# Six buffers of split weights placed 64 bytes apart modulo 512 in a float32r transformer trunk

## The chip, the cores and the metric

The kernel runs on one core of a Trainium2 chip. The metric is the device time of one execution in microseconds (us); the median of several runs is compared. Engines are named as the profile names them: PE multiplies matrices (PEld is its weight load, which overlaps), DVE, ACT and POOL work elementwise, SP issues the loads.

## What is computed

The reference is a decoder trunk of two pre-norm layers on 256 tokens of width 2048, all in float32. Layer 0 mixes tokens by sliding-window attention with sinks, layer 1 by a sparse attention with compressed, selected and window branches. Both have the same frame:

```python
def mixer_a(h, w_in, sinks, w_out, cos, sin):
    proj = h @ w_in
    q, k, v, z = jnp.split(proj, [A_WIDTH, A_WIDTH + A_KV_WIDTH, A_WIDTH + 2 * A_KV_WIDTH], axis=-1)
    ...
    return (o * jax.nn.silu(z)) @ w_out

def reference(...):
    for i in range(DEPTH):
        h = rmsnorm(x, norm_w[i])
        ...
        x = x + out.astype(x.dtype)
    return rmsnorm(x, final_norm_w)
```

The four big products (two `w_in`, two `w_out`) and the small compression network (mlp) of layer 1 read every weight once.

## The kernel before

Float32 products are made of float32r matmuls on operands split in two: `hi` is the value rounded to float32r, `lo` the rest. Weights come in steps of 128 x 1024 floats: SP loads one into `raw` (4 buffers), ACT writes `w_hi`, DVE writes `w_lo = raw - w_hi` (`split`, lines 558 to 569; 3 buffers each, the six buffers of this case), and PE uses both. The activations are split likewise into `hT` (the normed input) and `aT_hi`, `aT_lo` (the mixer's gated output).

A step is used in one of three ways. In "tok" steps (`add_steps`) a 128-column slice of `hT` or `aT` is the stationary operand and 512 columns of `w_hi`, `w_hi` again, and `w_lo` stream past it: three matmuls of 512 columns for each of two slices of tokens and two rows of weights. In "feat" steps (the gate z) the weights are stationary, 128 columns at a time, and `hT` streams: one matmul of 512 columns on `w_hi`, one of 256 on `w_lo`. The mlp streams 256 columns of weights past slices of `X`, which lie 488 bytes apart, and the attention scores stream `kTA` or `kTB` past `qT`. A row of `kTA` takes 2112 bytes (4 x 512 + 64), so its eight rows (four groups, hi and lo) start 64 bytes apart modulo 512, while `qT` starts at one fixed place.

Nothing is issued as it is written. Each call is recorded as an operation with the boxes of the tiles that it touches (`record`); two operations depend on each other where boxes overlap (`_overlap`). `order` then runs a list scheduler with estimated costs over all of them and writes the program in the order of its start times. For a slice of a tile the box is exact; for a slice of a slice `View.__getitem__` keeps the box of the first slice. The semaphores of the built program are made later from the real addresses.

`place` fixes where tiles lie: rings of tiles whose rows are a multiple of 512 bytes come first, from the longest to the shortest, then the others as they were recorded. So in the kernel before every tile with a row of 512 bytes or a multiple, the six weight buffers, `raw`, `hT`, `aT`, `kTA` and `qT` among them, starts at the same place modulo 512.

The first two steps are split in two halves each (`parts = 2`), since PE waits for them at the start; all others in one piece.

Of the kernel before, what the change touches and what calls it, by code (L numbers as in the profile page):

```python
# [13 lines left out]
F32R = mybir.dt.float32r  # L14
# [6 lines left out]
P = 128  # L21
# [318 lines left out]
def trunk(ctx: ExitStack, tc: tile.TileContext, x, final_norm_w, a_w_in, a_w_out, b_w_in, kc_pos, kc_w1, kc_w2, vc_pos, vc_w1, vc_w2,  # L340
# [5 lines left out]
    sb = Ring(plan, ctx.enter_context(tc.tile_pool(name="sb", bufs=1)))  # L346
# [15 lines left out]
    def copy(out, in_, scale=1.0):  # L362
        return ACT.activation(out, in_, AF.Copy, scale=scale)
# [195 lines left out]
    def split(st):  # L559
        n = st.cols  # L560
        plan.early = FIRST
        st.hi, st.lo = st.room() if hasattr(st, "room") else (
            sb.tile([P, 1024], F32R, tag=tag, name=tag, bufs=3) for tag in ("w_hi", "w_lo"))
        parts = 2 if st.idx < 2 else 1
        for c in range(parts):
            part = slice(c * n // parts, (c + 1) * n // parts)
            st.ops = (copy(st.hi[:, part], st.raw[:, part]),
                      DVE.tensor_sub(st.lo[:, part], st.raw[:, part], st.hi[:, part]))
        plan.early = 0
# [761 lines left out]
    for i in range(AHEAD):  # L1331
        split(steps[i])
    rates = [(0, 450.0), (nA, 900.0), (nA + 8, 600.0), (nA_out, 750.0), (nB, 1200.0)]
    for i, st in enumerate(steps):
        for start, r in rates:
            if i == start:
                state["rate"] = r
        if i == nA_out:
            mlp_loads()
        if i == nA + 8:  # L1340
            queue.append(pipeline(units, b_front, b_back))
        if i == 0:
            load_x(2)
        if i + LOADS < n:
            load(steps[i + LOADS])
        if i < 3:
            load_x((i + 3) % 4, steps[i + LOADS].load)
        if i + AHEAD < n:
            split(steps[i + AHEAD])
        for h in st.halves[:1] if i >= n - KT // 2 else st.halves:  # L1350
            h()
            background()
# [61 lines left out]
```

## Time and profile before

| | |
|---|---|
| median of 3 runs | 783.36 us (782.95 to 784.16) |
| the profiled execution | 783.71 us |
| its span in the profile | 781.6 us |
| PE busy | 767.5 us of the span (98%) |
| DVE, ACT, POOL busy | 569.7, 469.7, 123.5 us |

[...] Columns of each view are told where it first stands.

### The profile page before, as it was taken

How to read it: one execution, taken by the hardware profiler on the slowest of the kernel's cores; microseconds unless marked ns; L12 is line 12 of the kernel's file. 1: busy time of each engine (PE TensorE's matmuls, PEld its weight loads, DVE VectorE, ACT ScalarE, POOL GpSimd, SP SyncE). 2: the span in 40 equal slices, each digit the busy share in tenths (PEclk: the TensorE clock that was granted, in tenths of full speed). 3: DMA queues.
4: the chain of work that ended last, by engine and by line, in shares of the span. 5: the costliest groups of instructions: out<-in, count | busy, mean ns of one | idle time of the engine just before them, and what ended most of it. 6: DMA issues, size and time to landing. Idle time of an engine off the chain costs nothing.

```text
span 781.6 us, 11575 instructions
## 1 busy us (share of the span) xinstructions
PE 767.5 (98%) x3988; PEld 624.1 (80%) x3988; DVE 569.7 (73%) x1159; ACT 469.7 (60%) x950; POOL 123.5 (16%) x170
## 2 busy tenths in 40 slices
PE   8999999999999999999999999999999999999995
PEld 5888688788787788888888888878878887768884
DVE  5758959859779655556776479969969798965572
ACT  6847556457466444554666477657757866845442
POOL 1112112113023000020001020311132411111110
PEclk9999999999999999999999999999999999999998
DMA  9764454654553555666677664545445353464652
GB/s 326 241 187 137 140 185 110 182 176 127 172 176 116 184 185 187 188 191 176 188 241 234 169 170 116 155 115 156 120 131 141 109 160 104 131 193 150 195 168 107
DMA packets 86474, 129.73 MB, mean 166 GB/s; under 512 B 6322, under 2 KB 43233, under 8 KB 86288
## 3 DMA queue, kind: packets, MB, share of 16 engines
q1 hardware_dynamic: 85648, 127.16, 54.1%
q0 software_dynamic: 336, 1.29, 0.5%
q8 instruction: 31, 0.51, 0.3%
q10 hardware_dynamic: 432, 0.56, 0.2%
q14 instruction: 27, 0.22, 0.1%
HBM read 126.89 MB, written 2.10 MB: 165 GB/s over the span
## 4 chain that ended last, share of the span: by engine, by line
PE 83%; DVE 12%; issue 3%; DMA 1%; ACT 0%; ACTq 0%; POOLq 0%; POOL 0%; DVEq 0%
PE acc L217 68%; PE pv L217 4%; DVE w_lo L217 3%; PE s L217 3%; PE pT L217 3%; DVE sm L217 3%; DVE den L217 2%; DVE u L217 1%; PE mlp L217 1%; DVE qT L217 1%; PE qT L217 1%; PE gates L217 1%; PE xT L217 1%; DMA raw<-in_a_w_in 1%; DVE pt L217 1%
## 5 line engine op out<-in xcount | busy, mean ns | idle before, releaser
L217 DVE TENSOR_TENSOR w_lo<-raw,w_hi 128x1024 fp32r<-128x1024 f32 (+1 forms) x231 | 298.6, 1295 | 140.2 <-ACT w_hi L217 137.7
L217 ACT ACTIVATE w_hi<-raw 128x1024 fp32r<-128x1024 f32 (+1 forms) x231 | 241.1, 1048 | 161.5 <-PE acc L217 124.1
L217 PE MATMUL acc<-w_hi,hT 128*128 128x512 f32 x768 | 245.6, 396 | 2.8 <-ACT w_hi L217 1.8
L217 PE MATMUL acc<-hT,w_hi 128*128 128x512 f32 x512 | 185.0, 397 | 0.0
L217 PEld LDWEIGHTS acc<-w_hi,hT 128*128 128x128 f32 x768 | 142.5, 189 | 34.8 <-ACT w_hi L217 3.0
L217 PE MATMUL acc<-w_lo,hT 128*128 128x512 f32 x384 | 150.9, 395 | 0.0
L217 PE MATMUL acc<-hT,w_lo 128*128 128x256 f32 x512 | 144.8, 285 | 0.0
L217 PEld LDWEIGHTS acc<-hT,w_hi 128*128 128x128 f32 x512 | 96.2, 188 | 18.0
L217 PEld LDWEIGHTS acc<-hT,w_lo 128*128 128x128 f32 x512 | 96.6, 189 | 0.7
L217 PE MATMUL acc<-w_hi,aT_hi 128*128 128x512 f32 x236 | 92.5, 393 | 0.3 <-DVE kTB L217 0.3
L217 PE MATMUL acc<-w_hi,aT_lo 128*128 128x512 f32 x236 | 92.6, 392 | 0.0
L217 PE MATMUL acc<-w_lo,aT_hi 128*128 128x512 f32 x236 | 92.0, 391 | 0.0
L217 PEld LDWEIGHTS acc<-w_lo,hT 128*128 128x128 f32 x384 | 72.7, 189 | 13.7
L217 ACT ACTIVATE sm<-sm,nmb 128x128 f32<-128x128 f32 (+1 forms) x128 | 56.7, 444 | 18.6 <-DVE nmb L217 15.3
L217 POOL TENSOR_TENSOR sm<-sm,denb 128x512 f32<-128x512 f32 (+1 forms) x16 | 30.5, 1906 | 143.1 <-DVE denb L217 32.3
L217 PEld LDWEIGHTS acc<-w_hi,aT_hi 128*128 128x128 f32 x236 | 44.2, 188 | 9.9 <-DVE kTB L217 0.8
L217 PEld LDWEIGHTS acc<-w_hi,aT_lo 128*128 128x128 f32 x236 | 44.3, 188 | 9.7 <-issue 0.8
L217 PEld LDWEIGHTS acc<-w_lo,aT_hi 128*128 128x128 f32 x236 | 44.3, 188 | 9.0
L217 DVE CUSTOM_DVE_ANT_0 sm<-s,mask 128x128 f32<-128x128 f32 (+1 forms) x128 | 42.6, 347 | 10.1 <-PE s L217 9.6
L217 PE MATMUL pT<-ident,sm 128*128 128x128 f32 x256 | 38.2, 274 | 0.6 <-DVE sm L217 0.6
L217 PEld LDWEIGHTS s<-kTB,qT 128*128 128x128 f32 x192 | 31.9, 188 | 8.2 <-issue 3.1
L217 PE MATMUL s<-kTB,qT 128*128 128x272 f32 x192 | 38.3, 295 | 0.0
(188 smaller groups left out, 860.8 us busy)
## 6 DMA issues: line engine op xcount, KB each, us to landing
raw<-in_b_w_in SPq DMA_DIRECT2D x88, 512.0 KB, 3.7
raw<-in_a_w_in SPq DMA_DIRECT2D x71, 512.0 KB, 3.7
raw<-in_a_w_out SPq DMA_DIRECT2D x32, 512.0 KB, 4.5
raw<-in_b_w_out SPq DMA_DIRECT2D x32, 512.0 KB, 4.7
x<-in_x SPq DMA_DIRECT2D x8, 256.0 KB, 6.7
raw<-in_b_cmp_k_w SPq DMA_DIRECT2D x4, 512.0 KB, 3.8
raw<-in_b_cmp_v_w SPq DMA_DIRECT2D x4, 512.0 KB, 4.0
out<-x SPq DMA_DIRECT2D x4, 512.0 KB, 3.1
```

The lines of the kernel that those rows point to most:

```text
L217: return getattr(eng.real, method)(*[real(a) for a in args], **{k: real(a) for k, a in kw.items()})
```

## The change

Each of the six buffers gets 1040 floats a row instead of 1024, of which the first 1024 are used.

```diff
         st.hi, st.lo = st.room() if hasattr(st, "room") else (
-            sb.tile([P, 1024], F32R, tag=tag, name=tag, bufs=3) for tag in ("w_hi", "w_lo"))
+            sb.tile([P, 1040], F32R, tag=tag, name=tag, bufs=3)[:, 0:1024] for tag in ("w_hi", "w_lo"))
```

A row is now 4160 bytes, 8 x 512 + 64. It is no multiple of 512, so `place` puts the six buffers behind all the larger tiles, among the small ones. Counted in bytes modulo 512 the three `w_hi` start at 320, 384 and 448 and the three `w_lo` at 0, 64 and 128; before, all six started at 128, where `hT`, `aT`, `qT` and `kTA` still start. The larger tiles that stood behind the six move down by 24,576 bytes, a multiple of 512.

The `[:, 0:1024]` makes the buffer a slice, so the halves that `split` takes of it are slices of a slice and keep the box of all 1024 columns. In the first two steps the scheduler thus takes a matmul on the first half to wait for the second half too, and orders the program differently there; the semaphores, made from addresses, are as fine as before. Steps from the third on are written in one piece, and their order stays: of some 2,960 rows on PE the first 165 or so differ.

On PE, at the first step's matmuls. The tiles `acc0` and `acc1` are the sums of the two halves of the tokens; `w_hi_70`/`w_lo_71` and `w_hi_198`/`w_lo_207` are the first and second step's weights. Before:

```order
L217 MATMUL acc0_184<-w_hi_70,hT_63 128x512 x2
L217 MATMUL acc1_189<-w_hi_70,hT_63 128x512 x2
L217 MATMUL acc0_184<-w_lo_71,hT_63 128x512
L217 MATMUL acc1_189<-w_lo_71,hT_63 128x512
L217 MATMUL acc0_184<-w_hi_70,hT_63 128x512 x2
L217 MATMUL acc1_189<-w_hi_70,hT_63 128x512 x2
L217 MATMUL acc0_184<-w_lo_71,hT_63 128x512
L217 MATMUL acc1_189<-w_lo_71,hT_63 128x512
L217 MATMUL acc0_184<-w_hi_198,hT_63 128x512 x2
```

Now (`w_hi_105`/`w_lo_106` and `w_hi_190` are the same two steps):

```order
L217 MATMUL acc0_194<-w_hi_105,hT_63 128x512 x2
L217 MATMUL acc1_198<-w_hi_105,hT_63 128x512 x2
L217 MATMUL acc0_194<-w_lo_106,hT_63 128x512
L217 MATMUL acc0_194<-w_hi_105,hT_63 128x512 x2
L217 MATMUL acc0_194<-w_lo_106,hT_63 128x512
L217 MATMUL acc1_198<-w_lo_106,hT_63 128x512
L217 MATMUL acc1_198<-w_hi_105,hT_63 128x512 x2
L217 MATMUL acc1_198<-w_lo_106,hT_63 128x512
L217 MATMUL acc0_194<-w_hi_190,hT_63 128x512 x2
```

The first two matmuls on the weights' second half now stand ahead of the second one on `w_lo`'s first half.

On ACT, where it splits the second step (the difference of the two orders):

```order
 L217 ACTIVATE w_hi<-raw 128x512
 L217 ACTIVATE hT<-xf,small 128x256 x4
-L217 ACTIVATE w_hi<-raw 128x512 x3
+L217 ACTIVATE w_hi<-raw 128x512 x2
 L217 ACTIVATE hT<-xf,small 128x256 x2
+L217 ACTIVATE w_hi<-raw 128x512
 L217 ACTIVATE w_hi<-raw 128x1024 x2
```

The second half of the second step now stands behind two copies into `hT`; DVE's `w_lo` of that half moved likewise behind its two operations on `hT`.

## Rows read from the trace of the kernel before

**Rows 1.** Page, part 1: busy us (share of span) and instructions, by engine.

```profile
PE 767.5 (98%) x3988; PEld 624.1 (80%) x3988; DVE 569.7 (73%) x1159; ACT 469.7 (60%) x950; POOL 123.5 (16%) x170
```

**Rows 2.** Waits of PE: waiter, waited for, total us, times, longest.

```profile
PE acc L217 <- ACT w_hi L217: 1.8, 1, 1.8
...
PE pcT L217 <- DVE pc L217: 0.3, 1, 0.3
```

**Rows 3.** PE groups: out<-in, shape, count | busy us, mean ns | idle before.

```profile
L217 PE MATMUL acc<-w_hi,hT 128*128 128x512 f32 x768 | 245.6, 396 | 2.8 <-ACT w_hi L217 1.8 <-DVE u L217 1.0
L217 PE MATMUL acc<-hT,w_hi 128*128 128x512 f32 x512 | 185.0, 397 | 0.0
...
L217 PE MATMUL acc<-w_hi,aT_lo 128*128 128x512 f32 x236 | 92.6, 392 | 0.0
```

**Rows 4.** Timeline of PE, tok steps: start us, duration us, engine, out<-in, count.

```profile
212.18 0.39 PE L217 MATMUL acc<-w_lo,hT 128*128 128x512 f32 x1
212.40 0.61 PE L217 MATMUL acc<-w_hi,hT 128*128 128x512 f32 x2
212.86 0.39 PE L217 MATMUL acc<-w_lo,hT 128*128 128x512 f32 x1
```

**Rows 5.** Timeline of PE, feat steps in two stretches.

```profile
69.11 0.28 PE L217 MATMUL acc<-hT,w_lo 128*128 128x256 f32 x1
...
70.17 0.28 PE L217 MATMUL acc<-hT,w_lo 128*128 128x256 f32 x1
...
456.09 0.39 PE L217 MATMUL acc<-hT,w_hi 128*128 128x512 f32 x1
...
458.52 0.39 PE L217 MATMUL acc<-hT,w_hi 128*128 128x512 f32 x1
```

**Rows 6.** Timeline of PE, scores of group 3 and mlp.

```profile
233.92 0.63 PE L217 MATMUL s<-kTA,qT 128*128 128x256 f32 x4
234.39 0.28 PE L217 MATMUL acc<-hT,w_lo 128*128 128x256 f32 x1
...
414.77 0.28 PE L217 MATMUL mlp<-w_lo,X 128*122 128x256 f32 x1
...
415.59 0.39 PE L217 MATMUL acc<-w_lo,hT 128*128 128x512 f32 x1
```

**Rows 7.** Timeline of PE at the start, the first step's matmuls.

```profile
6.96 1.35 PE L217 MATMUL acc<-w_hi,hT 128*128 128x512 f32 x4 [1.83 <-ACT w_hi L217]
8.12 1.05 PE L217 MATMUL acc<-w_lo,hT 128*128 128x512 f32 x2
9.08 2.08 PE L217 MATMUL acc<-w_hi,hT 128*128 128x512 f32 x4
10.96 0.76 PE L217 MATMUL acc<-w_lo,hT 128*128 128x512 f32 x2
11.56 0.40 PE L217 MATMUL acc<-w_hi,hT 128*128 128x512 f32 x1
```

**Rows 8.** Timelines of ACT and DVE in the same stretch.

```profile
8.42 1.67 ACT L217 ACTIVATE w_hi<-raw 128x512 fp32r<-128x512 f32 x3
10.00 0.89 ACT L217 ACTIVATE hT<-xf,small 128x256 fp32r<-128x256 f32 x2
...
9.14 1.88 DVE L217 TENSOR_TENSOR w_lo<-raw,w_hi 128x512 fp32r<-128x512 f32 x3
10.94 0.87 DVE L217 SCALAR_TENSOR_TENSOR hT<-xf,small,hT 128x256 fp32r<-128x256 f32 x2
```

**Rows 9.** Windows: stretch, length; PE, PEld, DVE, ACT, POOL; PEclk, DMA share, GB/s.

```profile
7.90:9.10 1.20, 1.20 (x5) 0.47 (x3) 1.20 (x4) 1.20 (x4) 0.00 (x0) 0.50 1.05 405
9.10:11.00 1.90, 1.90 (x6) 1.51 (x6) 1.90 (x5) 1.82 (x5) 0.00 (x0) 0.50 1.05 391
11.00:11.60 0.60, 0.60 (x4) 0.52 (x3) 0.60 (x3) 0.60 (x1) 0.00 (x0) 0.79 1.04 382
```

**Rows 10.** Timeline of DVE, a split of keys.

```profile
38.52 0.69 DVE L217 TENSOR_TENSOR kTA<-kT,kTA 128x512 fp32r<-128x512 f32 x1 [2.69 <-ACT kTA L217]
```

## The prediction, made before the changed kernel ran

> **What bounds the kernel now.** I read the busy shares first, then the waits of PE, then its timeline. The busy shares [rows 1] show PE at 98% of the span and no other engine above 73%. The waits [rows 2] show what little PE stands idle for: six rows from 1.8 down to 0.3 us, 5.3 us together, and the two longest of them lie before the first real matmul. So the time is the number of matmuls times the distance between their starts, plus the start and the tail, and only something that changes that distance can move it by much.
>
> The distance is read from the timeline. In a tok step three matmuls of 512 columns take from 212.18 to 212.86 us [rows 4], 226.7 ns each. In a feat step a pair of 512 and 256 columns takes 353.3 ns where three pairs run from 69.11 to 70.17 us, and 347.1 ns where seven run from 456.09 to 458.52 us [rows 5]: the same instructions on the same places modulo 512 run in two rhythms. The counts [rows 3]: 768 tok matmuls on w_hi and half as many on w_lo, 1152; three groups of 236 in the output products (one row of them stands there), 708; 512 feat pairs. That is 2372 matmuls of 512 columns with a split weight on one side, and 512 of 256. At 226.7 ns the 2372 are 537.7 us. The second halves of the pairs are, at 347.1 - 226.7 = 120.4 ns, another 61.6 us. About 599 of the 781.6 us thus touch the six buffers, which is why an address effect, if there is one, would be large.
>
> **The change part by part.** It adds no instruction and no byte of traffic. It has three parts.
>
> First, the new places. What would a matmul cost when the streaming and the stationary operand start at different places modulo 512? The kernel before has such matmuls. The scores stream kTA, whose rows climb by 64 bytes, past qT, which stays. In group 3 they start 384 and 448 bytes ahead of qT: four of them take from 233.92 to 234.39 us [rows 6], 117.5 ns each. The mlp has its stationary slices 488 bytes apart, so all but a few differ from the streaming weights: seven take from 414.77 to 415.59 us [rows 6], 117.1 ns each. Both have 256 columns, as has the second of a feat pair, whose operands start at one place: 120.4 ns in the quiet rhythm. The unequal ones are no slower, and only 3 ns shorter, which is less than the two rhythms differ by. So I take zero for this part. Bounds: the 3 ns shorter on 2372 + 512 matmuls would give 8.7 us back; on the other side the rhythms show what a matmul can lose without any wait, (353.3 - 347.1) / 2 = 3.1 ns, or 8.9 us on the same count. Zero is nearest to the rows, since the group-3 scores climb the very same ladder of 64 bytes.
>
> The splits write the six buffers and DVE reads one of them. DVE's split of 512 columns of keys, which writes rows on that ladder, takes 0.69 us [rows 10]; its three splits of 512 columns of weights take 1.88 us together, 0.63 us each as they follow one another [rows 8]. A lone operation shows its full length and one in a row the distance, so these differ by less than 0.06 us. Even 0.1 us more on each split would be hidden: DVE has 27% of the span free [rows 1], and PE waits for no w_lo at all [rows 2]. If that cover were gone, each split would cost its excess once. Zero.
>
> Second, the new order on PE in the first step. Before, the two matmuls on the first half of w_lo start at 8.12, and the next on w_hi at 9.08 [rows 7]. That last start is set by ACT: the second half of w_hi is the first of three splits from 8.42 on, 0.56 us each [rows 8], so it is ready about 9.0. At half clock two matmuls fill 8.12 to 9.08 almost wholly: four take 9.08 to 10.96, so one is some 0.43 to 0.47 us. Now only one stands there, and PE then waits for the same 9.08: it idles some 0.43 us longer. The matmul that moved out of the gap runs at the end of the step instead, after 11.56, where the clock is full again and a matmul costs 0.23 us. So PE is 0.23 us later from there on. The matmul on the second half of w_lo is not late: DVE's first split ends at 9.14 + 0.63 = 9.8, two matmuls from 9.08 end at 10.0. Since PE has no waits behind it to absorb the 0.23 us, it reaches the end. Bounds: nothing (if ACT is earlier), and 0.5 us, the whole gap.
>
> Third, the new order on ACT and DVE in the second step. The second half of its split now comes two copies later on ACT, 0.89 us, and two operations later on DVE, 0.87 us [rows 8]; DVE ends it near 12.0 instead of 11.0. PE asks for it seven matmuls into the second step, at 11.8 + 7 x 0.23 = 13.4 us, so 1.4 us cover it. If they were gone it would cost up to 0.9 us. SP's load into the raw buffer of that step goes out up to 0.9 us later, with the pieces of x queued behind it, but the DMA engines are full in that stretch (DMA share 1.04 or more [rows 9]), so what waits is moved by the same queue anyway. The first transposes of x stand five matmuls earlier on PE; that is cheap if the pieces have landed, and I allow 0.3 us.
>
> The sum is made against the profiled execution: 783.71 us, of which 781.6 are the span and 2.1 lie around it. 783.71 + 0.23 = 783.94. The median of the runs shown is 0.35 us lower, so the forecast for the median is 783.36 + 0.23 = 783.6 us. One more thing moves without a cause that I can aim at: which rhythm the feat pairs fall into, 6.2 ns on each of 512 pairs, 3.2 us between all and none. The trace has both, so about 1.6 us either way.
>
> **The rivals.** (a) The operands do collide now, and the change frees them: faster. What a matmul costs beyond its columns is read from two sizes: 226.7 ns for 512 columns and 120.4 for 256 give 106.3 for 256 more columns, so 14.1 ns remain that are fixed. If all of it were collision, 2372 + 512 matmuls would give back 40.7 us: 742.9 us. Against it: the scores at 117.5 ns and the mlp at 117.1 still hold some 11 of those 14 ns at unequal places. For it: no row has 512 streaming columns at unequal places. A tenth of it is 4 us. [...]
>
> (b) Streaming from a start that is only a multiple of 64 costs something over 512 columns: slower. Its place is every tok and output matmul on the six buffers, 1860 of them; at the 3.1 ns above it is 5.8 us, 789.4 us. It decides from 1.57 / 1860 = 0.8 ns. The scores speak against it.
>
> [...]
>
> (d) The change doesn't do what it says, in effect: the third w_lo still starts at 128, where hT and aT start, so one of six buffers is unmoved. It gives the forecast's time, and the others a control.
>
> **How the numbers follow.** A measurement of this kernel can tell about 0.2%, 1.57 us, from no change. Forecast (783.6): 0.75, of which 0.04 falls on each side of the bound through the rhythms. Rival (a): 0.07, faster. (b): 0.07, slower. (c): 0.09, of which 0.07 slower and 0.02 within. (d): 0.02, within. So faster 0.11, same 0.71, slower 0.18. The range takes the forecast with its rhythms (782.0 to 785.2), the clock's case with some of them, and a small part of (a) and (b): 781.3 to 786.4 us. It leaves out the bulk of (a) and (b).
>
> **What would show it.** In the trace of the changed kernel three tok matmuls should again take 0.68 us, at every place of the buffers; three feat pairs 1.04 to 1.06. The first matmul on the second half of w_hi should start near 9.1 after an idle of about 0.5 us, and the second step's first matmul some 0.2 us later than now. PE should be busy about 767 us. [...] The prediction is wrong if the distance between matmuls depends on the start modulo 512 for 512 columns though it doesn't for 256, or if the six buffers' move among the small tiles meets something that no row of the kernel before could show.

## The result: slower by 0.66%

| | before | after |
|---|---|---|
| median of 4 runs | 783.53 us (782.95 to 784.16) | 788.27 us (788.14 to 788.87) |
| ratio, 95% interval | | 1.0066 (1.0054 to 1.0078) |
| the profiled execution | 783.71 us | 788.37 us |
| its span | 781.6 us | 786.3 us |

The time lies 4.7 us above the forecast and above the range. It is the outcome of rival (b), slower, at about its price (789.4 us).

The page of after, part 1, then PE's waits (waiter, waited for, total us, times, longest) and three of its groups (shape, count, busy us, mean ns, idle before):

```profile
PE 772.7 (98%) x3988; PEld 624.0 (79%) x3988; DVE 568.6 (72%) x1159; ACT 470.0 (60%) x950; POOL 124.8 (16%) x170
```

```profile
PE acc L217 <- ACT w_hi L217: 1.4, 1, 1.4
...
PE pcT L217 <- DVE pc L217: 0.3, 1, 0.3
```

```profile
L217 PE MATMUL acc<-w_hi,hT 128*128 128x512 f32 x768 | 248.0, 399 | 2.3 <-ACT w_hi L217 1.4
L217 PE MATMUL acc<-hT,w_hi 128*128 128x512 f32 x512 | 183.9, 395 | 0.0
...
L217 PE MATMUL acc<-w_hi,aT_lo 128*128 128x512 f32 x236 | 93.5, 396 | 0.0
```

PE is busy 5.2 us longer on the same 3988 matmuls [rows 1], and its six waits are no longer than before [rows 2]. No engine became a bound. The groups show where it went [rows 3]: those that stream w_hi grew (245.6 to 248.0 us, 92.6 to 93.5), the one in which w_hi stands still shrank (185.0 to 183.9). The timeline of PE in after, first and last row of one unbroken stretch of tok steps:

```profile
208.88 0.39 PE L217 MATMUL acc<-w_lo,hT 128*128 128x512 f32 x1
...
219.25 0.40 PE L217 MATMUL acc<-w_lo,hT 128*128 128x512 f32 x1
```

There are 45 matmuls from the first to the last: 10.37 us, 691 ns for three. Before it was 680 [rows 4].

A sum over the whole trace, from each matmul's start to the next one's, gives the budget. The 1152 tok matmuls on hT took 271.93 us before and 274.63 after, +2.70. The output products, all but the last of their 708, which has no next start to measure to, took 163.89 and 166.53, +2.63. The w_hi halves of the feat pairs took 120.81 and 119.89, -0.92; the w_lo halves are the same within 0.1. All else is +0.3 together, and the total is the 4.66 us between the two profiled executions. On the 1859 matmuls that stream the six buffers 5.33 us are 2.9 ns each; rival (b) had 3.1.

So the questions were: is it the places, or the new order and the new region of memory that came with them? If places, which: a start by itself, or a start relative to something, and to what? And can the gain in the feat pairs be had alone?

### The profile page after: what moved, and what is told of

The parts are those of the page before. It is cut to its first block, busy times and chain, and to the rows that moved or that the text cites. A ratio compares the mean times of both kernels' runs of the same rounds, so it can differ in the third digit from the quotient of the medians.

```text
span 786.3 us, 11576 instructions
## 1 busy us (share of the span) xinstructions
PE 772.7 (98%) x3988; PEld 624.0 (79%) x3988; DVE 568.6 (72%) x1159; ACT 470.0 (60%) x950; POOL 124.8 (16%) x170
## 4 chain that ended last, share of the span: by engine, by line
PE 83%; DVE 11%; issue 3%; DMA 1%; ACT 0%; ACTq 0%; POOLq 0%; POOL 0%; DVEq 0%
PE acc L217 69%; PE pv L217 4%; PE s L217 3%; DVE w_lo L217 3%; PE pT L217 3%; DVE sm L217 3%; DVE den L217 2%; DVE u L217 1%; PE mlp L217 1%; DVE qT L217 1%; PE qT L217 1%; PE gates L217 1%; PE xT L217 1%; DMA raw<-in_a_w_in 1%; DVE pt L217 1%
## 5 line engine op out<-in xcount | busy, mean ns | idle before, releaser
L217 DVE TENSOR_TENSOR w_lo<-raw,w_hi 128x1024 fp32r<-128x1024 f32 (+1 forms) x231 | 296.3, 1284 | 147.0 <-ACT w_hi L217 144.6
L217 ACT ACTIVATE w_hi<-raw 128x1024 fp32r<-128x1024 f32 (+1 forms) x231 | 241.1, 1048 | 168.1 <-PE acc L217 129.5
L217 PE MATMUL acc<-w_hi,hT 128*128 128x512 f32 x768 | 248.0, 399 | 2.3 <-ACT w_hi L217 1.4
L217 PE MATMUL acc<-hT,w_hi 128*128 128x512 f32 x512 | 183.9, 395 | 0.0
L217 PEld LDWEIGHTS acc<-w_hi,hT 128*128 128x128 f32 x768 | 142.8, 189 | 36.3 <-ACT w_hi L217 2.6
L217 PE MATMUL acc<-w_lo,hT 128*128 128x512 f32 x384 | 151.9, 397 | 0.0
L217 PE MATMUL acc<-hT,w_lo 128*128 128x256 f32 x512 | 144.4, 284 | 0.0
L217 PEld LDWEIGHTS acc<-hT,w_hi 128*128 128x128 f32 x512 | 96.3, 188 | 17.4
L217 PEld LDWEIGHTS acc<-hT,w_lo 128*128 128x128 f32 x512 | 96.3, 188 | 0.8 <-DVE w_lo L217 0.2
L217 PE MATMUL acc<-w_hi,aT_hi 128*128 128x512 f32 x236 | 93.2, 396 | 0.3 <-DVE kTB L217 0.3
L217 PE MATMUL acc<-w_hi,aT_lo 128*128 128x512 f32 x236 | 93.5, 396 | 0.0
L217 PE MATMUL acc<-w_lo,aT_hi 128*128 128x512 f32 x236 | 92.9, 394 | 0.0
L217 PEld LDWEIGHTS acc<-w_lo,hT 128*128 128x128 f32 x384 | 72.5, 189 | 14.6 <-DVE w_lo L217 0.3
L217 ACT ACTIVATE sm<-sm,nmb 128x128 f32<-128x128 f32 (+1 forms) x128 | 56.8, 445 | 18.4 <-DVE nmb L217 15.0
L217 POOL TENSOR_TENSOR sm<-sm,denb 128x512 f32<-128x512 f32 (+1 forms) x16 | 31.5, 1966 | 142.2 <-DVE mx L217 33.0
L217 PEld LDWEIGHTS acc<-w_hi,aT_hi 128*128 128x128 f32 x236 | 44.3, 188 | 10.8 <-DVE kTB L217 0.8
L217 PEld LDWEIGHTS acc<-w_hi,aT_lo 128*128 128x128 f32 x236 | 44.3, 188 | 10.5 <-issue 0.8
L217 PEld LDWEIGHTS acc<-w_lo,aT_hi 128*128 128x128 f32 x236 | 44.3, 188 | 9.8
L217 DVE CUSTOM_DVE_ANT_0 sm<-s,mask 128x128 f32<-128x128 f32 (+1 forms) x128 | 42.7, 348 | 10.1 <-PE s L217 9.8
L217 PE MATMUL pT<-ident,sm 128*128 128x128 f32 x256 | 38.1, 274 | 0.5 <-DVE sm L217 0.5
L217 PEld LDWEIGHTS s<-kTB,qT 128*128 128x128 f32 x192 | 31.9, 188 | 8.2 <-issue 3.1
L217 PE MATMUL s<-kTB,qT 128*128 128x272 f32 x192 | 38.3, 295 | 0.0
```

What stands on the lines that cost most here:

```text
L217: return getattr(eng.real, method)(*[real(a) for a in args], **{k: real(a) for k, a in kw.items()})
```

## Experiments

A streaming distance below is the time for three tok matmuls (w_hi, w_hi, w_lo), from start to start: the records themselves overlap, 0.39 us each where the starts stand 0.227 us apart [rows 4]. "Settled" means that at least 24 tok matmuls on hT ran just before and another follows; before's trace has 113 such triples, all at 680 ns. Each kernel's two timeline rows are the first and last of its unbroken tok stretch near 210 us, with the count from the first to the last behind them. In all kernels but the two last ones every buffer is a slice of a tile, as in after, so that the order is after's.

**Equal places again, with all else as in after.** The six buffers stay behind the larger tiles, and a pad in front puts all of them at 128 modulo 512, where hT and aT start. (Here and in the later edits the line of `place` that keeps the six there is left out.)

```diff
+    W_PAD = {"w_hi": 320, "w_lo": 0}
...
+        def wbuf(tag):
+            pad = W_PAD.pop(tag, 0)
+            if pad:
+                sb.tile([P, pad // 4], F32, name="pad_" + tag)
+            return sb.tile([P, 1024], F32R, tag=tag, name=tag, bufs=3)[:, 0:1024]
```

> The six buffers lie where the change puts them, among the small tiles, and the program has the changed kernel's order, but all six start at 128 modulo 512 like hT, aT and qT. Theory 'place': the loss comes from the unequal starts; settled tok rows are back at 680 ns per three matmuls and the time is near before, 783.5 to 784 us. Rival 'region or order': the move by 79 KB or the new order at the start costs it; 788 us, and tok rows stay at 691 to 700 ns per three.

Measured: 783.70 us, ratio 1.0007 (0.9998 to 1.0016).

```profile
208.77 0.39 PE L217 MATMUL acc<-w_lo,hT 128*128 128x512 f32 x1
...
217.61 0.39 PE L217 MATMUL acc<-w_lo,hT 128*128 128x512 f32 x1
```

39 matmuls in 8.84 us, 680 ns for three. The loss is gone with the new order and the new region still in place. It is the places; order and region together cost at most 0.16%, the upper end of the interval.

**All six at 192,** 64 bytes past hT and aT, with nothing unequal among them.

```diff
+    W_PAD = {"w_hi": 384, "w_lo": 0}
```

> As a_equal_late, but all six start at 192, 64 bytes off hT and aT and equal among themselves. If unequal starts of one stream and the next cost the time (streams of w_hi, w_hi, w_lo following one another), nothing is unequal there in a tok step: 680 ns per three, 783.5 us. If the streaming operand against the stationary one counts, every tok matmul is 64 off: 688 ns or more per three, 786 to 790 us.

Measured: 787.05 us, ratio 1.0042 (1.0026 to 1.0059).

```profile
208.97 0.39 PE L217 MATMUL acc<-w_lo,hT 128*128 128x512 f32 x1
...
219.96 0.40 PE L217 MATMUL acc<-w_lo,hT 128*128 128x512 f32 x1
```

48 matmuls in 10.99 us, 687 for three. So the buffers needn't differ from each other to lose; it is enough that they differ from something that stayed.

**The same 192 with everything else shifted too.** A pad of 64 bytes ahead of all tiles; buffers, hT, aT and the rest all start at 192.

```diff
+    front = sb.tile([P, 16], F32, name="front")
...
+    W_PAD = {"w_hi": 320, "w_lo": 0}
```

> A pad of 64 bytes ahead of everything: all large tiles, the six buffers, hT, aT, qT and kTA's base start at 192 instead of 128. If only relations between operands count, 680 ns per three and 783.5 to 784 us. If a start at an odd multiple of 64 costs in itself, 688 ns or more per three and 786 to 790 us.

Measured: 783.90 us, ratio 1.0007 (0.9998 to 1.0017).

```profile
208.73 0.39 PE L217 MATMUL acc<-w_lo,hT 128*128 128x512 f32 x1
...
218.93 0.39 PE L217 MATMUL acc<-w_lo,hT 128*128 128x512 f32 x1
```

45 matmuls in 10.20 us, 680 for three. A start at 192 costs nothing by itself. That corrects rival (b), which put the cost on the start.

**w_hi at 320, w_lo at 128,** to see hi and lo apart.

```diff
+    W_PAD = {"w_hi": 0, "w_lo": 320}
```

> The three w_hi start at 320, the three w_lo at 128 like hT and aT. In the changed kernel's trace a feat pair whose w_hi starts at 320 and whose w_lo starts at 128 takes 340 ns most often, against 350 in the mean of before. If that pair cost follows the places, all 512 feat pairs take 340 to 343 ns, 3.5 to 5 us less than before. Tok rows: if unequal places cost, 229 to 234 ns a matmul as for these two places in the changed kernel, 4 to 9 us more than before. So 783 to 788 us; if places do not matter by themselves, 783.5 with feat pairs at 347 to 353.

Measured: 791.81 us, ratio 1.0108 (1.0093 to 1.0123).

```profile
208.68 0.40 PE L217 MATMUL acc<-w_lo,hT 128*128 128x512 f32 x1
...
220.65 0.39 PE L217 MATMUL acc<-w_lo,hT 128*128 128x512 f32 x1
```

51 matmuls in 11.97 us, 704 for three, although one of the three streams from an equal place: hi and lo don't simply add, and the time lies above the 783 to 788 us expected. In the feat pairs the same places gain. By the budget their w_hi halves take 1.84 us less than before and the w_lo halves 0.61 less, and 209 of 392 pairs in a row take 340 ns, as only six of before's 392 do.

**The ladder of distances.** All six at one place; only the pad differs. At 320, 384 and 0 they stand 192, 256 and 384 bytes past hT and aT (modulo 512); 448 and 64, run later, are 320 and 448 past them. The lines stand in this order.

```diff
+    W_PAD = {"w_hi": 0, "w_lo": 0}
+    W_PAD = {"w_hi": 64, "w_lo": 0}
+    W_PAD = {"w_hi": 192, "w_lo": 0}
+    W_PAD = {"w_hi": 128, "w_lo": 0}
+    W_PAD = {"w_hi": 256, "w_lo": 0}
```

> As c_all192, with all six at 320: streams equal among themselves, 192 bytes ahead of the stationary hT and aT. If only the distance between the streaming and the stationary operand counts, the w_hi of e_hi320_lo128 have the same distance, so settled rows are between 693 and 707 ns per three and the time 788 us or more. If the change from one stream's place to the next counts as well, as e_hi320_lo128 had it and c_all192 not, rows are near the 687 ns of c_all192 and the time near 787 us.

> All six at 384, half of 512 ahead of hT and aT. If distance counts smoothly, half is the farthest: more than the 687 ns per three of c_all192 and 788 us or more. If any unequal place costs the same, 687 ns and 787 us.

> All six at 0, 384 ahead of hT and aT (128 behind). If the side counts (streaming ahead or behind), this differs from c_all192: near 680 ns per three and 783.5 us, or 693 and more and 789 us. If any unequal place costs the same, 687 ns and 787 us.

> The kernel before with all six buffers at 448 modulo 512, 320 bytes from the operands that stand still, which is 64 modulo 256. Theory (the period is 256 bytes): as c_all192, 687 ns per three settled tok matmuls, 786.5 to 787.5 us. Rival (the period is 512, and g_all384 was equal by the place 256 alone): some other rhythm, 690 ns or more, 789 us or above.

> The kernel before with all six buffers at 64 modulo 512, 448 bytes from the operands that stand still, which is 192 modulo 256. Theory (the period is 256 bytes): as f_all320, 697 to 703 ns per three, 791 to 792.5 us. Rival (the cost grows with the distance in either direction, so that 64 bytes below is the same as 64 bytes above): as c_all192, 687 ns per three and 787 us.

At 320, 48 matmuls in 11.19 us:

```profile
209.03 0.39 PE L217 MATMUL acc<-w_lo,hT 128*128 128x512 f32 x1
...
220.22 0.39 PE L217 MATMUL acc<-w_lo,hT 128*128 128x512 f32 x1
```

At 384, 39 in 8.84:

```profile
209.23 0.39 PE L217 MATMUL acc<-w_lo,hT 128*128 128x512 f32 x1
...
218.07 0.39 PE L217 MATMUL acc<-w_lo,hT 128*128 128x512 f32 x1
```

At 0, 48 in 11.15:

```profile
208.69 0.39 PE L217 MATMUL acc<-w_lo,hT 128*128 128x512 f32 x1
...
219.84 0.40 PE L217 MATMUL acc<-w_lo,hT 128*128 128x512 f32 x1
```

At 448, 42 in 9.61:

```profile
209.08 0.39 PE L217 MATMUL acc<-w_lo,hT 128*128 128x512 f32 x1
...
218.69 0.39 PE L217 MATMUL acc<-w_lo,hT 128*128 128x512 f32 x1
```

At 64, 51 in 11.90:

```profile
208.83 0.40 PE L217 MATMUL acc<-w_lo,hT 128*128 128x512 f32 x1
...
220.73 0.39 PE L217 MATMUL acc<-w_lo,hT 128*128 128x512 f32 x1
```

| buffers past hT, aT modulo 512 | modulo 256 | settled, per matmul | time |
|---|---|---|---|
| 0 (before, and the two shifts above) | 0 | 226.67 ns | 783.5 to 783.9 us |
| 256 | 0 | 226.67 | 783.67 |
| 64 | 64 | 228.97 | 787.05 |
| 320 | 64 | 228.97 | 786.28 |
| 384 | 128 | 232.5 | 790.58 |
| 192 | 192 | 233.3 | 792.03 |
| 448 | 192 | 233.3 | 792.61 |

The times from the second row on, but for 787.05, are of one execution each. Places 256 bytes apart give the same distance to about a hundredth of a nanosecond and times within 0.8 us: in steps of 64 bytes the period is 256. That 384 would cost nothing was neither of the two cases expected for it. The sign counts: 64 bytes behind (448, that is 192 modulo 256) costs 6.7 ns, 64 bytes ahead 2.3.

**The stationary operand moved instead.** The six buffers stay at 128; hT, aT and kTA go to 192, and raw, from which ACT and DVE fill the buffers, stays equal to the buffers modulo 256. In all earlier runs both relations had changed together.

```diff
+    front = sb.tile([P, 16], F32, name="front")
+    mid = sb.tile([P, 48], F32, name="mid")
...
+    W_PAD = {"w_hi": 64, "w_lo": 0}
```

> The kernel before with the six buffers left at 128 modulo 256, as in before, and the operands that stand still (hT, aT, kTA) moved to 192 instead; the loaded rows raw that are split into the six buffers stay equal to them modulo 256. Theory (only streaming minus stationary place modulo 256 counts; here it is minus 64, which is 192): the settled rows of tok as in f_all320, 697 to 703 ns per three, and the time about 791 to 792 us. Rival (what counts is how the six buffers lie against the rows raw from which ScalarE and VectorE fill them, which moved together with the places in all the runs so far): 680 ns per three and 783.5 us.

Measured: 792.56 us in one execution.

```profile
209.16 0.39 PE L217 MATMUL acc<-w_lo,hT 128*128 128x512 f32 x1
...
220.36 0.39 PE L217 MATMUL acc<-w_lo,hT 128*128 128x512 f32 x1
```

48 matmuls in 11.20 us, 700 for three, the row of 192 in the table. It is what TensorE reads, streaming place minus stationary place modulo 256. The place of the buffers against raw, where the splits of ACT and DVE read, has no part that shows: the time is that of 64 and 320 (792.61 and 792.03 us), where both relations had moved.

**The gain alone.** From before, w_hi is moved by 192 bytes in the feat steps only; tok and output steps keep equal places. For that the three w_hi become slots of one tile, 1152 floats apart. First try:

```diff
+            o = 1152 * (W_HI[1] % 3) + (48 if st.feat else 0)
+            W_HI[1] += 1
+            st.hi = W_HI[0][:, o:o + 1024]
```

> From the kernel before: everything starts at 128 as there, but in feat steps alone, where weights are stationary, w_hi is written and read 192 bytes further on (at 320), w_lo stays. If places of the operands are the cause step by step, tok rows keep 680 ns per three, feat pairs fall to 340 ns as in e_hi320_lo128 (343.9 in the mean against 350.1), 512 x 6.2 ns = 3.2 us less at most, 2.5 us as measured there: 780.3 to 781.2 us. If the feat pairs of e_hi320_lo128 gained only because the tok steps beside them were slow, 783.5 us.

Measured: 784.15 us, ratio 1.0010 (1.0000 to 1.0019). The feat pairs went to 343.3 ns in the mean, 2.7 us less by the budget, but the time did not fall. The slice of a slice had changed the order of the first steps, as in the change itself. PE's timeline at the start:

```profile
7.12 1.22 PE L217 MATMUL acc<-w_hi,hT 128*128 128x512 f32 x2 [1.42 <-ACT w_hi L217]
8.14 0.63 PE L217 MATMUL acc<-w_lo,hT 128*128 128x512 f32 x1
9.24 1.22 PE L217 MATMUL acc<-w_hi,hT 128*128 128x512 f32 x2 [0.47 <-ACT w_hi L217]
10.25 0.63 PE L217 MATMUL acc<-w_lo,hT 128*128 128x512 f32 x1
10.68 1.05 PE L217 MATMUL acc<-w_hi,hT 128*128 128x512 f32 x2
...
12.81 0.63 PE L217 MATMUL acc<-w_lo,hT 128*128 128x512 f32 x1
13.24 0.93 PE L217 MATMUL acc<-w_hi,hT 128*128 128x512 f32 x2
14.01 0.40 PE L217 MATMUL acc<-w_lo,hT 128*128 128x512 f32 x1
```

PE idles 0.47 us ahead of 9.24, and until 13.24 its matmuls stand 0.43 us apart, twice the later distance; before they did so only until about 11 [rows 7]. The budget has +2.01 us in the tok matmuls on hT, where the settled ones are unchanged at 680. So 2.0 of the 2.7 us were paid back at the start; another 0.5 stands in the matmuls on pt, as in the second try below. A gap, then a longer stretch at about half the rate: before had its half rate where the granted clock was 0.50 [rows 9], but here PEclk reads 1.00 in every window from 7.0 to 14.5 us, so that it is the clock is not shown.

Second try: a small class hands out the slice with its exact box, so that the scheduler sees the halves apart and PE's first 1,900 matmuls come in the order of before; 97 of the later ones, all before the 2,200th, change places.

```diff
+class Slot:
+    def __getitem__(self, idx):
+        p, s = idx
+        return self.base[p, self.o + s.start:self.o + s.stop]
...
+            st.hi = Slot(W_HI[0], o)
```

> The kernel before, but in the steps of kind feat alone, where the split weights stand still and the gathered rows hT stream, w_hi lies 64 bytes off modulo 256 (at 192) and w_lo stays at 128; tok, out and all else lie as before, and the first 700 matmuls of TensorE come in the order of before. Theory (what a feat pair costs is set by the places of w_hi, w_lo and hT modulo 256, and the loss of the earlier try of this lay in its changed start alone): tok rows settled at 680 ns per three, feat pairs at 343 to 344 ns as in h_feat_hi192, which is 392 pairs by some 6.5 ns, 2.5 us; the start as before (idle before the first hT matmuls and granted clock alike); time 780.3 to 781.5 us against 783.5, ratio 0.996 to 0.998. Rival (the feat stretch is bound by something else, the loads of w or the ring's splitting, and the gain of the pairs comes back as waits): feat pairs 343 ns but PE waits longer by 2 us or more, time 783 us or above.

Measured: 781.08 us (8 runs) against 783.09, ratio 0.9975 (0.9964 to 0.9985): faster than both kernels. Its page, two of its groups, a stretch of feat steps and the start (the code stands nine lines lower, so L217 is L226):

```profile
PE 765.0 (98%) x3988; PEld 622.9 (80%) x3988; DVE 569.1 (73%) x1159; ACT 470.1 (60%) x950; POOL 123.9 (16%) x170
```

```profile
L226 PE MATMUL acc<-w_hi,hT 128*128 128x512 f32 x768 | 245.2, 396 | 3.3 <-ACT w_hi L226 2.1
L226 PE MATMUL acc<-hT,w_hi 128*128 128x512 f32 x512 | 182.0, 393 | 0.0
```

```profile
60.37 0.39 PE L226 MATMUL acc<-hT,w_hi 128*128 128x512 f32 x1
...
63.44 0.39 PE L226 MATMUL acc<-hT,w_hi 128*128 128x512 f32 x1
```

```profile
7.04 1.73 PE L226 MATMUL acc<-w_hi,hT 128*128 128x512 f32 x4 [2.08 <-ACT w_hi L226]
8.57 1.06 PE L226 MATMUL acc<-w_lo,hT 128*128 128x512 f32 x2
9.42 1.77 PE L226 MATMUL acc<-w_hi,hT 128*128 128x512 f32 x4
11.03 0.62 PE L226 MATMUL acc<-w_lo,hT 128*128 128x512 f32 x2
```

Nine pairs take 3.07 us, 341 ns each, where before three took 1.06 and seven 2.43, 353 and 347 [rows 5]. The budget of the feat pairs is 2.69 us below before's; the tok group is as before, and the start no longer pays it back. Of the 2.69 us the profiled executions show 1.79 and the medians 2.01. PE's waits are 0.8 us longer in all (the longest 2.1 us instead of 1.8, those for u 1.2 instead of 1.0 together), so a part of the gain comes back as waiting; and 0.55 us more stand in the matmuls on pt, for a reason that was not tried.

## Why the prediction was wrong

**What bounds the kernel** was right. PE is at 98% and its waits are no more than before, so the time moved with the distance between matmuls and with nothing else.

**"First, the new places" is the step that failed.** It asked the right question and answered it from the scores and the mlp, which have 256 streaming columns [rows 6], for matmuls of 512. The rows were read rightly: in before's trace the scores on kTA at 0, 64, 128 and 192 past qT modulo 256 follow one another at 118.5, 117.4, 118.8 and 118.0 ns in the mean (63 distances), so there the place makes no difference that shows. They don't carry over: over 512 columns it makes 2.3 to 6.7 ns [rows 4 against the table]. Two things differ, and no run separates them: the scores have 256 columns, and they come in bursts of a few matmuls. The size alone is not a safe reason, since the second matmul of a feat pair, 256 columns in a long stretch, does pay: from its start to the next one's it takes 117.1 ns before, and 118.3, 119.6 and 118.9 with all six buffers 64, 128 and 192 past hT (450 distances each). The prediction noted that no row had 512 columns at unequal places and still gave the rival that rests on it 0.07. Its bound from the two rhythms, 3.1 ns, was close to the 2.9 that came; it should have carried more of the chance, since nothing in the profile spoke against it at this size.

The rival that came true, (b), had the place and the price, but not the relation. A start at 192 is as good as one at 128 if the stationary operand is there too; only the difference modulo 256 counts.

Part (d) said that the w_lo left at 128 would be a control. It is a weak one: after's settled triples were 686 to 707 ns, never 680, since no step of it has both w_hi and w_lo at equal places. Nor do the three matmuls add up: w_hi at 192 past hT with w_lo at 0 past it takes 234.5 ns a matmul, where two thirds of 6.7 would give 231.1; with w_lo at 128 past it, in after, 229.7, less than the table has for either place. What a matmul pays also depends on its neighbours' places. How was not settled.

Rival (a), that the new places free something, was not right for the kernel as a whole, but in the feat pairs there is such a gain; that it is a collision undone is not shown. The gain needs w_hi off and w_lo on the place of hT: with all six off by 192 the pairs stay at 350 ns (350.0 before), with w_hi alone off they fall to 343.4, most of them to 340. After has both kinds: with w_lo on and w_hi 192 or 64 past hT its pairs take 342.9 and 345.1 ns, with w_hi on and w_lo off 349.2. The term "which rhythm the feat pairs fall into" (1.6 us either way) was thus in part a matter of places, and gave the change 1.0 us back.

**The splits' cost, zero,** was right: DVE's splits take 296.3 us in all (298.6 before), ACT's 241.1 in both.

**"Second, the new order on PE": 0.23 us,** came out at nothing in after's profiled execution. PE's start there:

```profile
7.12 2.07 PE L217 MATMUL acc<-w_hi,hT 128*128 128x512 f32 x4 [1.41 <-ACT w_hi L217]
8.99 0.63 PE L217 MATMUL acc<-w_lo,hT 128*128 128x512 f32 x1
9.41 1.05 PE L217 MATMUL acc<-w_hi,hT 128*128 128x512 f32 x2
...
11.55 1.09 PE L217 MATMUL acc<-w_hi,hT 128*128 128x512 f32 x4
```

The second step's first matmul starts at 11.55, before at 11.56 [rows 7]. The idle 0.43 us that the step expected is not there. The first four matmuls now take 1.87 us instead of 1.16, because they already run at the wide distance, and so ACT's second half is ready when PE comes to it. The windows of this stretch (length; busy of PE, PEld, DVE, ACT, POOL; PEclk, DMA share, GB/s) can't say why:

```profile
7.00:9.00 2.00, 1.89 (x5) 1.49 (x5) 1.91 (x5) 2.00 (x6) 0.00 (x0) 1.00 1.06 407
9.00:10.86 1.86, 1.86 (x6) 1.28 (x5) 1.86 (x4) 1.86 (x5) 0.00 (x0) 1.00 1.05 387
```

Their PEclk is 1.00 where the matmuls stand 0.43 to 0.47 us apart, while before showed 0.50 at that distance [rows 9], and so does the faster kernel:

```profile
7.50:10.50 3.00, 3.00 (x9) 2.27 (x8) 3.00 (x8) 3.00 (x7) 0.00 (x0) 0.50 1.06 397
```

But the trace of after holds no record of the clock ahead of 10.53 us, where one of 1.00 begins, and the column is 1.00 where there is no record. So the clock of the wide stretch in after is not shown.

That the idle is missing is luck of the execution, not of the order. The first and the third experiment (equal places, and everything shifted) have after's order, and in their traces it is there, 0.69 us long. The rows of the first step's start, of the matmuls behind the idle and of the second step's start, in the first and then in the third experiment:

```profile
6.80 1.20 PE L217 MATMUL acc<-w_hi,hT 128*128 128x512 f32 x4 [1.49 <-ACT w_hi L217]
...
8.92 0.73 PE L217 MATMUL acc<-w_hi,hT 128*128 128x512 f32 x2 [0.69 <-ACT w_hi L217]
...
11.00 1.08 PE L217 MATMUL acc<-w_hi,hT 128*128 128x512 f32 x4
```

```profile
6.94 1.20 PE L217 MATMUL acc<-w_hi,hT 128*128 128x512 f32 x4 [1.25 <-ACT w_hi L217]
...
9.06 1.22 PE L217 MATMUL acc<-w_hi,hT 128*128 128x512 f32 x2 [0.69 <-ACT w_hi L217]
...
12.21 1.16 PE L217 MATMUL acc<-w_hi,hT 128*128 128x512 f32 x4
```

From the first step's first matmul to the second's it is 4.20 us in the one and 5.27 in the other, against 4.43 in after and 4.60 before [rows 7]. So one order took from 0.4 us less to 0.7 us more than before, and the 0.23 us were too small a term to be told; the ratio of 1.0007 (at most 1.0016) with after's order bounds it. A long stretch at the wide distance behind the gap came in the third experiment and in the first try of the gain alone, where it lasted two microseconds longer than before; in the first experiment the gap came without it. What decides was not settled.

**The clock's case,** (c) of the chances with 0.09 and a part of the range, rests on a term that no run shows. In its place the traces show that the clock of before came back to 1.00 within 11.00 to 11.60 us [rows 9] and that after's was at 1.00 from 10.53 us on at the latest, so it rose no later there.

**"Third, the new order on ACT and DVE"** cost nothing that shows: the budget outside the six buffers is +0.3 us in all.

## What to carry to other kernels

On a TensorE-bound float32r kernel, keep the start of what streams and the start of what stands still equal modulo 256 bytes where 512 columns of weights stream; here a buffer's pad of 64 bytes, harmless by every count of instructions and bytes, cost 0.66%, and the worst place 1.2% (one execution). Where the weights stand still and activations stream, try the other places: one of them gave 0.25%. And don't carry a duration from one shape to another in a question about addresses: the short bursts of 256 columns did not show what 512 columns pay.

## What the runs showed of the hardware

The distance between settled float32r matmuls of 512 columns, each with its own weight load (3988 of each [rows 1]), depends in this kernel on streaming minus stationary place modulo 256 bytes: 226.67 ns at 0, and 2.3, 5.8 and 6.7 ns more at 64, 128 and 192 (seven places of the streaming operand, and one move of the stationary one). At 64 nearly all settled triples take 686 or 687 ns, one step of 6.7 ns more than 680; by the 106.3 ns that 256 more columns take (226.7 less 120.4), that is an estimated 16 columns, or 64 bytes of a row. At the other places they spread from 690 to 707.

Why the two places bear on each other no run shows; what is measured is the relation, of up to 6.7 ns on 226.67, 3%.

After a change from one kind of matmul to another the distance needs some matmuls to settle. In before's trace 84 of the 174 tok triples on hT with fewer than 24 tok matmuls ahead of them take 680 ns and the others 684 to 708, at equal places throughout (11 more, over 770 ns, are left aside); with fewer than 6 ahead the mean is 231.0 ns a matmul, from 18 on it is 226.67. With all six at 192 past, the unsettled triples take 233.3 like the settled ones. So an unsettled matmul loses 4.3 ns there in the mean (229.0 before) and a settled one 6.7, which is why 6.7 ns on 1859 matmuls, 12.5 us, became only 8.4 us by the budget (tok +4.59, output +3.81).
